# A two-layer sparse-attention trunk: values of a head pair later, softmax's last pass on ScalarE

## The chip, the cores and the metric

The kernel runs on one core of a Trainium2 chip. The metric is the device time of one execution in microseconds. TensorE does the matrix products, VectorE, ScalarE and GpSimd the elementwise work, and all DMAs of the part in question are issued from SyncE's queue (SP).

## The reference

512 positions, width 1024, two layers. Each layer norms its rows, multiplies by one wide input matrix, and sends the result through two branches: a sparse attention of 8 heads (here the change is) and a gated linear attention. Both are gated, projected up, summed, projected out, normed and added to the input. Cut to what matters:

```python
q_rope, k_slc, k_win = rope(...)                  # 8 heads in 2 groups, 64 wide
p_c = masked_softmax(q_nope @ k_cmp * scale)      # compressed keys, at most 31
p_s = masked_softmax(q_rope @ k_slc * scale)      # "selected" branch
p_w = masked_softmax(q_rope @ k_win * scale)      # "window" branch
o   = gate0 * p_c @ v_cmp + gate1 * p_s @ v_slc + gate2 * p_w @ v_win
o_nsa = o * silu(p_nz)
y   = m_nsa * (o_nsa @ w_up_nsa) + m_gla * (o_gla @ w_up_gla)
out = x + rms(y @ w_out, g_post)
```

With 512 positions there are 8 key blocks and up to 16 may be chosen, and the window is 512 wide, so both branches come to plain causal softmax over all earlier keys, with keys and values of their own.

## The kernel before

Matrices are split into a high and a low part in a short float format, and a product of two of them is three matmuls (`split3`): high by high, and the two mixed ones. Weights come by DMA into one of 3 `raw` buffers; ScalarE casts the high half (`hl`, line 153) and VectorE subtracts to get the low half (line 154), after which the raw buffer is free. They are read two blocks ahead. TensorE's instructions run in the order in which the program writes them; the orders on ScalarE, VectorE, GpSimd and SP are laid out by the framework's scheduler, which goes by priority and by its own estimate of times. Each engine then works its list off in order.

Attention goes by four **pairs** of heads, p and p + 4, and for a pair through five **blocks**: the compressed branch (`cmp_steps`, m = 0), then four of `attn_steps(p, ip, br)`: first half of the queries (ip 0) with branch 0 and 1 (m = 1, 2), second half (ip 1) with branch 0 and 1 (m = 3, 4). Such a block has two score units, i = 2 ip and 2 ip + 1, and then its value products:

- `scores`: four matmuls for 128 queries against (i + 1) x 128 keys, both heads; the unit i = 0 does both branches at once and holds the second one's result. It ends in `weigh` and `turn`.
- `weigh`, for one head at a time: VectorE adds the mask and takes the extreme of each row (line 970), ScalarE takes the exponential with its sum (line 972), VectorE takes the reciprocal (974) and multiplies each row by it and by the head's gate (975).
- `turn`: VectorE transposes 32 x 32 squares into a tile `T` (935); when both units of a block are there, SP writes `T` to DRAM (`tp`, 940) and reads it back with partitions regrouped (`PT`, four DMAs, 943).
- the value products (line 998): 8 TensorE instructions for a block of ip 0, 16 for one of ip 1, into an accumulator `acc` in a PSUM pool `ps_o` of one buffer. After the last block of a pair, line 1003 reads `acc` and multiplies by the gate, ScalarE casts the high part (1005), GpSimd subtracts for the low part (1006).

Between these, `fill(us)` writes steps of independent work into TensorE's order: the remaining query and gate projections, and the other branch's up-projections (`up`), three matmuls for 0.64 of credit. The main loop over 20 blocks writes out the order by hand: `go(n)` takes block n one step on. `PT` and `T` have tags by ip, `PT` with two buffers each, `T` with one. After the loop, `need("ug7")` writes the rest of the filler, then two gate projections of the next stage, the value products of the last pair's blocks 3 and 4, and the up-projection `un0` that reads the attention output of all four pairs in turn.

Of the kernel before, what the change touches and what calls it, by code (L numbers as in the profile page):

```python
# [9 lines left out]
F32 = mybir.dt.float32  # L10
# [3 lines left out]
AF = mybir.ActivationFunctionType  # L14
OP = mybir.AluOpType
# [6 lines left out]
NEG = -1e30  # L22
# [45 lines left out]
def trunk(ctx, tc, x, wpk, sp, gvec, cs, wa, out):  # L68
# [23 lines left out]
    def new(pl, shape=(128, 512), dt=F32, tag=None, bufs=None):  # L92
        cnt[0] += 1
        kw = {} if bufs is None else {"bufs": bufs}
        return sb[pl].tile(list(shape), dt, tag=tag or pl, name=f"{tag or pl}_{cnt[0]}", **kw)

    def ps(tag):
        cnt[0] += 1
        return psp[tag].tile([128, 512], F32, tag=tag, name=f"ps_{tag}_{cnt[0]}")
# [4 lines left out]
    mm, tp = nc.tensor.matmul, nc.tensor.transpose  # L104
    V, A, G = nc.vector, nc.scalar, nc.gpsimd
# [65 lines left out]
    def get(l, n, ahead=2):  # L171
        issue(POS[l, n] + ahead)
        return ready.pop((l, n))

    def split3(o, w, h, first, last):

        mm(o, w[0], h[0], start=first, stop=False)  # L177
        mm(o, w[0], h[1], start=False, stop=False)  # L178
        mm(o, w[1], h[0], start=False, stop=last)  # L179
# [132 lines left out]
    for l in range(L):  # L312
# [21 lines left out]
        def fill(us):  # L334
            credit[0] += us
            while credit[0] > 0.3 and queue:
                credit[0] -= step(*queue[0])

        def step(name, gen):
            try:  # L340
                return next(gen)
            except StopIteration:
                queue.pop(0)
                done.add(name)
                return 0.0

        def need(name):
            while name not in done:
                step(*queue[0])
# [3 lines left out]
        gt = new("sm", (128, 4, 24), tag="gt", bufs=1)  # L353
# [152 lines left out]
        if l == 0:  # L506
            with all_but_pe:
                ident_b, cmask, pmask, valid, gmask, kbd, vbd, hidk, hidv, cos, sin = first_stage()
# [34 lines left out]
        for t in range(2):  # L543
            o = ps("s")
# [148 lines left out]
        PR = [[None, None, None, None] for _ in range(4)]  # L693
# [37 lines left out]
        def up(f, gate, wn, src, then):  # L731
            th = []

            def sig(o):
                th.append(new("th"))
                A.activation(th[0], o, AF.Tanh, scale=0.5)

            yield from fm(l, f"{gate}{f}", hT, sig)
            w = get(l, f"{wn}{f}")
            u = ps("mm")  # L740
            for k in range(4):
                sl = slice(k * 128, (k + 1) * 128)
                split3(u, (w[0][:, sl], w[1][:, sl]), src[k], k == 0, k == 3)
                if k == 3:
                    then(th[0], u)
                yield 0.64
# [31 lines left out]
        for f in range(8):  # L778
            put(f"ug{f}", up(f, "mgg", "ug", oTg, take_ug))
# [142 lines left out]
        PT, TT, held, back, nsc = {}, {}, {}, [], [0]  # L922

        def turn(p, br, i, pps):

            ip, n = i // 2, i + 1
            r = (4 * ip + 3) * 64
            if i % 2 == 0:  # L930
                TT[p, br] = new("T", (128, 4, r), tag=f"T{ip}")
            T = TT[p, br]
            t = T[:, :, (i % 2) * i * 64:((i % 2) * i + n) * 64].rearrange("p b (j g q) -> p b j g q", j=n, g=2)
            for g in range(2):
                V.transpose(t[:, :, :, g], pps[g][:, :n * 128].rearrange("p (j b q) -> p b j q", j=n, b=4))  # L935
            if i % 2:
                cnt[0] += 1
                dr = dram.tile([128, 4, r], F32, tag=f"tp{ip}", name=f"tp_{cnt[0]}", bufs=2)
                with tc.issue_after(back[-1]) if back else nullcontext():
                    dma(dr, T)  # L940
                W = PT[p, br, ip] = new("PT", (128, 4, r), tag=f"PT{ip}")
                for b in range(4):
                    back.append(dma(W[b * 32:(b + 1) * 32], dr[:, b].rearrange("(a k) r -> k a r", a=4)).ins)

        def scores(p, i, brs):

            w = (i + 1) * 128
            ww = w * len(brs)  # L950
            both = len(brs) > 1
            nsc[0] += 1
            o = [ps("ts"[nsc[0] % 2]) for _ in range(2)]
            for g in range(2):
                for n in range(2):
                    kn = first[g][:, n].rearrange("p b n -> p (b n)") if both else keys[brs[0]][g][n][:, :w]
                    mm(o[g][:, :ww], PR[p][1][g][:, i * 128:(i + 1) * 128], kn, start=(n == 0), stop=(n == 1))  # L957
            pps = [weigh(p, g, i, brs, o[g]) for g in range(2)]
            turn(p, brs[0], i, [t[0] for t in pps])
            if both:  # L960
                held[p] = [t[1] for t in pps]

        def weigh(p, g, i, brs, o):
            h, w = p + 4 * g, (i + 1) * 128
            out = []
            for n, br in enumerate(brs):
                ob = o[:, n * w:(n + 1) * w]
                sx = new("sm", (128, 4), tag="sx", bufs=8)
                pp = new("g")
                V.tensor_tensor_reduce(pp[:, :w], ob, cmask[:, 512 - w:512], 1.0, -3 * NEG,  # L970
                                       OP.add, OP.min, sx[:, 0:1])
                A.activation(pp[:, :w], pp[:, :w], AF.Exp, bias=sx[:, 0:1], scale=-1.0,  # L972
                             accum_out=sx[:, 1:2])
                V.reciprocal(sx[:, 2:3], sx[:, 1:2])
                V.tensor_scalar(pp[:, :w], pp[:, :w], sx[:, 2:3],  # L975
                                gt[:, i, h * 3 + 1 + br:h * 3 + 2 + br], op0=OP.mult, op1=OP.mult)
                out.append(pp)
            return out

        def attn_steps(p, ip, br):  # L980
            for i in (2 * ip, 2 * ip + 1):
                if i or not br:
                    scores(p, i, (br,) if i else (0, 1))
                else:
                    turn(p, br, i, held.pop(p))
                yield

            acc, W = PR[p][3], PT[p, br, ip]
            i0 = 2 * ip
            for j in range(i0 + 2):  # L990
                for g in range(2):
                    c0 = br * 128 + g * 64
                    if j <= i0:
                        m = W[:, :, :2 * (i0 + 1) * 64].rearrange("p a (i j g q) -> p i a j g q", i=2, g=2, q=32)
                        m, w = m[:, :, :, j, g], 256
                    else:
                        m, w = W[:, :, (2 * j) * 64 + g * 32:(2 * j) * 64 + g * 32 + 32], 128
                    mm(acc[g * 64:(g + 1) * 64, (i0 + 2) * 128 - w:(i0 + 2) * 128],  # L998
                       vsw[j // 2][:, j % 2, c0:c0 + 64], m,
                       start=False, stop=(br == 1 and j == i0 + 1), skip_group_check=True)  # L1000
            if ip == 1 and br == 1:
                f_ = new("p")
                V.scalar_tensor_tensor(f_, acc, 0.5, PR[p][2], op0=OP.mult, op1=OP.mult)
                H, Lo = new("oT", dt=F32R), new("oT", dt=F32R)
                A.copy(H, f_)  # L1005
                G.tensor_tensor(Lo, f_, H.bitcast(F32), op=OP.subtract)  # L1006
                oTn[p] = (H, Lo)
            yield

        steps = []  # L1010
# [5 lines left out]
        def go(n):  # L1016
            if 0 <= n < len(steps):
                next(live[n])
# [19 lines left out]
        for n in range(len(steps)):  # L1038
            m = n % 5
            f4 = FILL[m]  # L1040
            if m == 0:
                need(f"q{steps[n][0]}")
            if m == 4:
                need(f"nz{steps[n][0]}")
            go(n)
            if m == 3:
                go(n - 5)
                go(n - 4)
            fill(f4[0])
            if m == 2:  # L1050
                go(n - 2)
            fill(f4[1])
            if m != 0:
                go(n)
                fill(f4[2])
            if m == 3:
                go(n - 3)
            if m == 4:
                go(n - 3)
                go(n - 2)  # L1060
            fill(f4[3])
        need("ug7")

        uns = [up(f, "mgn", "un", oTn, take_un(f)) for f in range(8)]
# [10 lines left out]
        src = x if l == 0 else x1  # L1075
# [6 lines left out]
        for s in range(ST):  # L1082
# [4 lines left out]
            o = [ps("s" if s % 2 and n < 2 else "mm") for n in range(len(pieces))]  # L1087
# [17 lines left out]
            for h, c0, c1 in pieces:  # L1105
                V.scalar_tensor_tensor(xh[h][:, c0:c1], tt[h][:, c0:c1], rs[:, 0:1], xh[h][:, c0:c1],  # L1106
                                       op0=OP.mult, op1=OP.add)
# [80 lines left out]
```

## Time and profile before

| what | us |
|---|---|
| median of 3 runs (lowest, highest) | 810.62 (809.73, 812.09) |
| the profiled execution's own time | 808.68 |
| its span, first to last instruction | 807.0 |
| TensorE busy | 789.5 (98%) |
| VectorE busy | 553.5 (69%) |
| ScalarE busy | 354.4 (44%) |
| GpSimd busy | 97.6 (12%) |

A matmul counts as busy from its start until its result is written, and matmuls overlap, so an engine that is 98% busy may still start its matmuls late; the distance of starts tells. The attention parts of the two layers lie at about 148 to 306 and 543 to 702 us. TensorE's granted clock was 0.997 of full speed in the mean, 1.00 in the attention parts.

### The profile page before, as it was taken

The page shows a single profiled execution, that of the slowest core. Times are in us where ns is not written, and L with a number is a line of the kernel's source. Part 1 is how long each engine was busy: PE and PEld are TensorE (multiplying, and loading weights), DVE is VectorE, ACT ScalarE, POOL GpSimd, SP SyncE. Part 2 cuts the span into 40 slices and gives each one's busy share as a digit, 9 for nine tenths or more (in the row PEclk, how much of TensorE's full clock was granted, in tenths as well). Part 3 has the DMA queues.
Part 4 walks back from the last instruction along what each step waited for, and adds up shares of the span by engine and source line. Part 5 has one row for each costly group of instructions (what it writes and reads, how often), then busy time and mean ns, then how long its engine had stood idle before and what let it go on. Part 6 is the DMA issues. An engine that isn't in the chain of part 4 may idle for free. (4 is left out here: it accounts for less than half of the span.)

```text
span 807.0 us, 12043 instructions
## 1 busy us (share of the span) xinstructions
PE 789.5 (98%) x4262; PEld 644.4 (80%) x4262; DVE 553.5 (69%) x1274; ACT 354.4 (44%) x731; POOL 97.6 (12%) x117
## 2 busy tenths in 40 slices
PE   8999999999989999999999999999999999999996
PEld 5888788887878887888898878888877788788885
DVE  6753749999998945645574366589999987366223
ACT  5671236554554524442356413556555444245211
POOL 3000024000010102211010102311000101032100
PEclk9999999999999999999999999999999999999998
DMA  6641124367676773446246121234767677545222
GB/s 233 229 147 58 53 67 130 105 191 217 183 236 204 235 227 119 153 153 223 79 129 212 52 78 54 83 114 149 223 201 215 214 212 222 171 157 158 78 105 79
DMA packets 54272, 124.04 MB, mean 154 GB/s; under 512 B 6562, under 2 KB 23490, under 8 KB 54212
## 3 DMA queue, kind: packets, MB, share of 16 engines
q1 hardware_dynamic: 54064, 123.01, 48.4%
q8 instruction: 34, 0.56, 0.3%
q10 hardware_dynamic: 148, 0.27, 0.1%
q14 instruction: 26, 0.21, 0.1%
HBM read 94.94 MB, written 25.17 MB: 149 GB/s over the span
## 5 line engine op out<-in xcount | busy, mean ns | idle before, releaser
L177 PE MATMUL ps_mm<-hT,hl 128*128 128x512 f32 x544 | 217.5, 400 | 0.0
L178 PE MATMUL ps_mm<-hT,hl 128*128 128x512 f32 x544 | 212.5, 391 | 0.0
L179 PE MATMUL ps_mm<-hT,hl 128*128 128x512 f32 x544 | 212.3, 390 | 0.0
L153 ACT CAST hl<-raw 128x1024 fp32r<-128x1024 f32 (+3 forms) x107 | 97.6, 915 | 138.3 <-PE ps_mm L178 99.9
L154 DVE TENSOR_TENSOR hl<-raw,hl 128x1024 fp32r<-128x1024 f32 (+3 forms) x107 | 117.4, 1098 | 47.6 <-ACT hl L153 42.5
L177 PEld LDWEIGHTS ps_mm<-hT,hl 128*128 128x128 f32 x544 | 102.2, 188 | 23.3 <-issue 3.1
L179 PEld LDWEIGHTS ps_mm<-hT,hl 128*128 128x128 f32 x544 | 102.2, 188 | 22.1
L178 PEld LDWEIGHTS ps_mm<-hT,hl 128*128 128x128 f32 x544 | 102.4, 188 | 19.0
L972 ACT ACTIVATE g<-g,sx 128x128 f32<-128x128 f32 (+3 forms) x128 | 71.0, 555 | 67.9 <-DVE sx L970 67.5
L935 DVE STREAM_TRANSPOSE T<-g 128x256 f32<-128x256 f32 (+3 forms) x128 | 58.6, 491 | 0.7
L975 DVE TENSOR_SCALAR g<-g,sx,gt 128x128 f32<-128x128 f32 (+3 forms) x128 | 57.0, 459 | 1.5
L178 PE MATMUL ps_mm<-oT,hl 128*128 128x512 f32 x128 | 50.3, 393 | 1.7 <-POOL oT L1006 1.7
L177 PE MATMUL ps_mm<-oT,hl 128*128 128x512 f32 x128 | 50.9, 398 | 0.0
L179 PE MATMUL ps_mm<-oT,hl 128*128 128x512 f32 x128 | 49.9, 390 | 0.0
L1006 POOL TENSOR_TENSOR oT<-p,oT 128x512 fp32r<-128x512 f32 x8 | 14.3, 1784 | 239.0 <-ACT oT L1005 239.0
L998 PE MATMUL ps_o<-PT,a 128*64 128x256 f32 (+1 forms) x384 | 38.6, 348 | 3.9 <-DMA PT<-tp 3.9
L998 PEld LDWEIGHTS ps_o<-PT,a 128*64 128x64 f32 x384 | 25.4, 137 | 18.3 <-issue 9.4
L200 POOL TENSOR_TENSOR rs<-ms,mhalf 128x1 f32<-128x1 f32 (+1 forms) x24 | 17.2, 719 | 177.0 <-DVE ms L198 175.3
L1026 POOL TENSOR_TENSOR p<-p,g 128x512 f32<-128x512 f32 x16 | 28.0, 1750 | 84.3 <-DVE p L1025 72.7
L970 DVE CUSTOM_DVE_ANT_0 g<-ps_t,cmask 128x256 f32<-128x256 f32 (+3 forms) x64 | 28.8, 477 | 2.3 <-PE ps_t L957 2.2
L970 DVE CUSTOM_DVE_ANT_0 g<-ps_s,cmask 128x128 f32<-128x128 f32 (+3 forms) x64 | 29.0, 481 | 1.7 <-PE ps_s L957 1.7
L178 PEld LDWEIGHTS ps_mm<-oT,hl 128*128 128x128 f32 x128 | 24.1, 188 | 6.5 <-POOL oT L1006 2.3
(269 smaller groups left out, 1313.3 us busy)
## 6 DMA issues: line engine op xcount, KB each, us to landing
raw<-wpk SPq DMA_DIRECT2D x96, 512.0 KB, 3.8
tp<-T SPq DMA_DIRECT2D x16, 896.0 KB, 4.1
PT<-tp SPq DMA_DIRECT2D x64, 224.0 KB, 4.9
raw<-wpk SPq DMA_DIRECT2D x32, 256.0 KB, 3.0
tp<-T SPq DMA_DIRECT2D x16, 384.0 KB, 2.5
PT<-tp SPq DMA_DIRECT2D x64, 96.0 KB, 2.4
a<-wpk SPq DMA_DIRECT2D x16, 256.0 KB, 5.7
p<-x SPq DMA_DIRECT2D x16, 256.0 KB, 2.9
```

The costliest lines, as they stand in the source:

```text
L153: A.copy(H[:, :w], r[:, :w])
L154: V.tensor_tensor(Lo[:, :w], r[:, :w], H[:, :w].bitcast(F32), op=OP.subtract)
L177: mm(o, w[0], h[0], start=first, stop=False)
L178: mm(o, w[0], h[1], start=False, stop=False)
L179: mm(o, w[1], h[0], start=False, stop=last)
L200: G.tensor_tensor(r[:, :n], ms[:, :n], mhalf[:, :n], op=OP.pow)
L935: V.transpose(t[:, :, :, g], pps[g][:, :n * 128].rearrange("p (j b q) -> p b j q", j=n, b=4))
L970: V.tensor_tensor_reduce(pp[:, :w], ob, cmask[:, 512 - w:512], 1.0, -3 * NEG, OP.add, OP.min, sx[:, 0:1])
L972: A.activation(pp[:, :w], pp[:, :w], AF.Exp, bias=sx[:, 0:1], scale=-1.0, accum_out=sx[:, 1:2])
L975: V.tensor_scalar(pp[:, :w], pp[:, :w], sx[:, 2:3], gt[:, i, h * 3 + 1 + br:h * 3 + 2 + br], op0=OP.mult, op1=OP.mult)
L998: mm(acc[g * 64:(g + 1) * 64, (i0 + 2) * 128 - w:(i0 + 2) * 128], vsw[j // 2][:, j % 2, c0:c0 + 64], m, start=False, stop=(br == 1 and j = ...
L1026: G.tensor_tensor(t_, t_, y2[f], op=OP.add)
```

## The change

It has four pieces. The main loop's order: the value products of a pair's first two `attn_steps` blocks (m = 1, 2) move from the end of its block m = 4 to the first gap of the next pair's block m = 0 (for the last pair: behind the loop); those of its last two blocks (m = 3, 4) move from behind the first score unit of the next pair's m = 3 to in front of its second score unit. `weigh` now does both heads of a unit and one branch in a call: one reciprocal and one product with the gates for both heads, on 128 x 2, and the multiplication of the rows by ScalarE (`A.mul`) in place of VectorE. The end of a pair: line 1003 gets high priority in the scheduler, and for the last pair VectorE, not GpSimd, subtracts the low part. In `up`, the product with the low half of the source comes last of the three.

```diff
@@ up
-                split3(u, (w[0][:, sl], w[1][:, sl]), src[k], k == 0, k == 3)
+                mm(u, w[0][:, sl], src[k][0], start=(k == 0), stop=False)
+                mm(u, w[1][:, sl], src[k][0], start=False, stop=False)
+                mm(u, w[0][:, sl], src[k][1], start=False, stop=(k == 3))
@@ scores, weigh
-            pps = [weigh(p, g, i, brs, o[g]) for g in range(2)]
-            turn(p, brs[0], i, [t[0] for t in pps])
+            pps = [weigh(p, i, br, [o[g][:, n * w:(n + 1) * w] for g in range(2)]) for n, br in enumerate(brs)]
+            turn(p, brs[0], i, pps[0])
             if both:
-                held[p] = [t[1] for t in pps]
-
-        def weigh(p, g, i, brs, o):
-            h, w = p + 4 * g, (i + 1) * 128
-            out = []
-            for n, br in enumerate(brs):
-                ob = o[:, n * w:(n + 1) * w]
-                sx = new("sm", (128, 4), tag="sx", bufs=8)
-                pp = new("g")
-                V.tensor_tensor_reduce(pp[:, :w], ob, cmask[:, 512 - w:512], 1.0, -3 * NEG,
-                                       OP.add, OP.min, sx[:, 0:1])
-                A.activation(pp[:, :w], pp[:, :w], AF.Exp, bias=sx[:, 0:1], scale=-1.0,
-                             accum_out=sx[:, 1:2])
-                V.reciprocal(sx[:, 2:3], sx[:, 1:2])
-                V.tensor_scalar(pp[:, :w], pp[:, :w], sx[:, 2:3],
-                                gt[:, i, h * 3 + 1 + br:h * 3 + 2 + br], op0=OP.mult, op1=OP.mult)
-                out.append(pp)
-            return out
+                held[p] = pps[1]
+
+        def weigh(p, i, br, o):
+
+            w = (i + 1) * 128
+            sx = new("sm", (128, 8), tag="sx", bufs=4)
+            pps = [new("g") for _ in range(2)]
+            for g, pp in enumerate(pps):
+                V.tensor_tensor_reduce(pp[:, :w], o[g], cmask[:, 512 - w:512], 1.0, -3 * NEG,
+                                       OP.add, OP.min, sx[:, g:g + 1])
+                A.activation(pp[:, :w], pp[:, :w], AF.Exp, bias=sx[:, g:g + 1], scale=-1.0,
+                             accum_out=sx[:, 2 + g:3 + g])
+            V.reciprocal(sx[:, 4:6], sx[:, 2:4])
+            V.tensor_mul(sx[:, 6:8], sx[:, 4:6], gt[:, i, 3 * p + 1 + br:3 * p + 14 + br:12])
+            for g, pp in enumerate(pps):
+                A.mul(pp[:, :w], pp[:, :w], sx[:, 6 + g:7 + g])
+            return pps
@@ attn_steps
                 f_ = new("p")
-                V.scalar_tensor_tensor(f_, acc, 0.5, PR[p][2], op0=OP.mult, op1=OP.mult)
+                with tc.high_priority():
+                    V.scalar_tensor_tensor(f_, acc, 0.5, PR[p][2], op0=OP.mult, op1=OP.mult)
                 H, Lo = new("oT", dt=F32R), new("oT", dt=F32R)
                 A.copy(H, f_)
-                G.tensor_tensor(Lo, f_, H.bitcast(F32), op=OP.subtract)
+                (G if p < 3 else V).tensor_tensor(Lo, f_, H.bitcast(F32), op=OP.subtract)
@@ main loop
             go(n)
+            fill(f4[0])
+            if m == 0:
+                go(n - 4)
+                go(n - 3)
+            if m == 2:
+                go(n - 2)
+            fill(f4[1])
             if m == 3:
                 go(n - 5)
                 go(n - 4)
-            fill(f4[0])
-            if m == 2:
-                go(n - 2)
-            fill(f4[1])
             if m != 0:
                 go(n)
                 fill(f4[2])
+            fill(f4[3])
             if m == 3:
                 go(n - 3)
-            if m == 4:
-                go(n - 3)
-                go(n - 2)
-            fill(f4[3])
+        go(len(steps) - 4)
+        go(len(steps) - 3)
         need("ug7")
```

## Rows read from the trace of the kernel before

**Rows 1.** Windows by pair: us; busy PE, PEld, DVE, ACT, POOL; clock, DMA.
```profile
...
174.60:211.00 36.40, 36.40 (x200) 29.11 (x199) 34.66 (x105) 18.78 (x48) 2.85 (x2) 1.00 0.73 214
...
211.00:249.60 38.60, 36.54 (x200) 29.32 (x199) 36.50 (x110) 19.46 (x49) 2.15 (x1) 1.00 0.66 209
...
605.10:643.40 38.30, 36.43 (x200) 29.19 (x199) 36.31 (x110) 19.84 (x50) 2.16 (x1) 1.00 0.66 212
...
```

**Rows 2.** Waits of TensorE, whole span: us in total, times, longest us.
```profile
...
PE ps_o L998 <- DMA PT<-tp: 3.9, 2, 2.1
...
PE ps_mm L178 <- POOL oT L1006: 1.7, 2, 0.8
...
```

**Rows 3.** Timeline of one weight block: start, us, engine, line, operation.
```profile
...
209.34 1.03 ACT L153 CAST hl<-raw 128x1024 fp32r<-128x1024 f32 x1
...
213.95 1.22 DVE L154 TENSOR_TENSOR hl<-raw,hl 128x1024 fp32r<-128x1024 f32 x1
...
218.71 0.40 PE L177 MATMUL ps_mm<-hT,hl 128*128 128x512 f32 x1
...
```

**Rows 4.** Timeline of SP's queue, 207 to 226 us.
```profile
...
207.58 8.00 SPq L136 DMA_DIRECT2D raw<-wpk  x2
...
215.68 1.80 SPq L943 DMA_DIRECT2D PT<-tp  x4
...
225.40 1.80 SPq L943 DMA_DIRECT2D PT<-tp  x4
...
```

**Rows 5.** Timeline of TensorE and VectorE around the first wait.
```profile
...
232.29 1.74 PE L998 MATMUL ps_o<-PT,a 128*64 128x256 f32 x16 [2.06 <-DMA PT<-tp]
...
235.44 0.65 DVE L1003 SCALAR_TENSOR_TENSOR p<-ps_o,oT 128x512 f32<-128x512 f32 x1
...
239.78 0.39 PE L918 MATMUL ps_o<-p,vbd 128*128 128x512 f32 x1
...
```

**Rows 6.** VectorE: line 975 in three periods, then groups by shape.
```profile
...
sum 111.40, DVE 21.82; mean DVE 7.27
...
L975 DVE TENSOR_SCALAR g<-g,sx,gt 128x512 f32<-128x512 f32 x16 | 8.3, 531 | 0.1
...
L974 DVE RECIPROCAL sx<-sx 128x1 f32<-128x1 f32 x64 | 9.4, 155 | 3.4 <-ACT g L972 3.2
...
L726 DVE TENSOR_TENSOR oT<-p,oT 128x512 fp32r<-128x512 f32 x3 | 2.1, 684 | 0.0
...
```

**Rows 7.** ScalarE groups by shape: count, busy us, mean ns, idle before.
```profile
...
L972 ACT ACTIVATE g<-g,sx 128x512 f32<-128x512 f32 x16 | 11.5, 717 | 8.0 <-DVE sx L970 8.0
...
L972 ACT ACTIVATE g<-g,sx 128x128 f32<-128x128 f32 x16 | 6.2, 391 | 6.2 <-DVE sx L970 6.2
...
L698 ACT ACTIVATE a<-ps_mm 128x512 f32<-128x512 f32 x3 | 1.7, 580 | 0.0
...
```

**Rows 8.** Timelines of three engines at the last pair's end, first layer.
```profile
...
303.11 3.25 PE L998 MATMUL ps_o<-PT,a 128*64 128x256 f32 x32
...
308.01 0.39 PE L178 MATMUL ps_mm<-oT,hl 128*128 128x512 f32 x1
...
308.23 0.39 PE L179 MATMUL ps_mm<-oT,hl 128*128 128x512 f32 x1
...
308.52 0.50 PE L177 MATMUL ps_mm<-oT,hl 128*128 128x512 f32 x1
...
309.87 0.50 PE L178 MATMUL ps_mm<-oT,hl 128*128 128x512 f32 x1 [0.84 <-POOL oT L1006]
...
307.13 0.69 DVE L1003 SCALAR_TENSOR_TENSOR p<-ps_o,oT 128x512 f32<-128x512 f32 x1
...
308.54 1.27 POOL L1006 TENSOR_TENSOR oT<-p,oT 128x512 fp32r<-128x512 f32 x1 [33.40 <-ACT oT L1005]
...
```

**Rows 9.** DMA issues: count, KB each, median us to landing.
```profile
...
tp<-T SPq DMA_DIRECT2D x8, 896.0 KB, 4.1
...
PT<-tp SPq DMA_DIRECT2D x32, 224.0 KB, 5.0
...
```

## The prediction

> **What bounds the kernel now.** I read the stretches by head pair first, then the list of who TensorE waits for, then the order of time around each of its waits, on the DMA queue, VectorE and ScalarE, and last the durations of the operations that move. In the attention part each pair takes a period of 36.40 us in which TensorE shows 36.40 us busy; VectorE is busy for 34.66 us of it, 95%, and ScalarE for 18.78 us, 52% [rows 1]. One period of each layer is longer: 38.60 us, with 36.54 us busy, in the first and 38.30 us in the second [rows 1]. So TensorE is the bound, and a change to the softmax is worth only the TensorE waits that it takes away. The list has two kinds inside attention: the value products of line 998 for the transposed weights that come back from memory, 3.9 us in two waits, and the up-projection for the low half of the attention output that GpSimd makes on line 1006, 1.7 us in two [rows 2]. That is the whole ground to be won.
>
> The first wait goes back to VectorE. The high half of a weight block is ready when ScalarE's 1.03 us from 209.34 end, at 210.4; VectorE begins the low half only at 213.95, because it is working off softmax [rows 3]. SP's queue is in order: from 207.58 to 215.58 it stands at two weight loads that need a raw buffer which that low half, ending at 215.17, frees. Only then, at 215.68, does it issue the loads of the transposed weights for branch 0 of the pair's second half of queries, and at 225.40 those for branch 1 [rows 4]. The value products of that branch 1 start at 232.29, after 2.06 us of waiting [rows 5].
>
> **The change part by part.** *Softmax's last pass.* VectorE loses line 975, 7.27 us per period in the mean [rows 6]. Of 16 reciprocals of 155 ns per period [rows 6] 8 stay, each for two heads, and 8 products on 128x2 come. At this size the start-up is all there is, so I price a product as a reciprocal, and the two cancel; twice that would add 1.2 us. VectorE goes from 34.66 to about 27.5 us, 75% of the period. ScalarE gets 16 multiplications per period by a factor that differs by partition, four of each width from 128 to 512. The trace has none; the nearest are its multiplication by a constant, 580 ns at 512, and the exponential that also reads a value per partition, 717 ns at 512 and 391 at 128 [rows 7]. The upper bound is the exponential's, a mean of 554 ns: 16 x 0.554 = 8.9 us. The lower takes 580 ns at 512 and the exponential's slope, 109 ns per 128 columns: 4 x (580 + 471 + 362 + 254) ns = 6.7 us. I take 8.9 because of the operand. ScalarE then has 18.78 + 8.9 = 27.7 us, 76% of the period. Neither passes TensorE's 36.40, so this part costs TensorE nothing by itself; what hides it is the filler work between score units.
>
> The Trainium skill (ScalarE: Activation LUTs, "Rules for kernel authors") speaks against this part: it wants multiplications on VectorE. On one instruction the rows agree, 531 ns for line 975 at 512 columns against 580 to 717 [rows 6, 7]. By that page's formula ("What ACT_TABLE_LOAD costs": 186 ns + 0.833 ns per column, and 93 ns for a pointer operand), an estimate for 16 passes at a mean of 320 columns is 8.7 us, which leaves the sum as it is.
>
> *Latency of a unit.* The chain was sums, exponential, reciprocal, scaling, transposes, head by head; now both heads' exponentials come before one reciprocal, then a product (about 0.16), then ScalarE and back. Two passes of at most 0.72 replace two of about 0.53, and one head waits for the other: about 1 us more in an idle machine (an estimate from [rows 6, 7]). A gain is possible too, since VectorE's backlog, 3.6 us in the case above, shrinks.
>
> *Values later.* The same 16 and 32 value products run, no more and no fewer group changes, and no DMA is added. A pair's first units go from the end of its last block to the first gap of the next pair, 2.6 us of filler and the compressed scores later. The last ones go 1.5 + 1.2 = 2.7 us of filler later in the fourth block of the next pair. Against a wait of 2.06 us this alone, less the 1 us of latency, leaves 0.3 us; the shorter backlog, which freed the raw buffer 3.6 us late, takes more than that. I take the wait as gone: 3.9 us [rows 2]. The bounds are 0 (the next part, rival B) and 3.9.
>
> What may be late next is the accumulator, of which there is one: a new pair's first product on it (239.78) must follow the read of line 1003, which ended at 236.1 [rows 5]. After the change only four scores (4 x 0.23 us) and 3.3 us of filler, about 4.3 us, lie between. In the old order the read began 1.4 us after the products ended and took 0.65, so 2.2 us of cover stay, and the raised priority adds to them. I cost it at nothing; if VectorE is over 2.2 us late, every excess is TensorE's.
>
> *The end of the last pair.* TensorE's matmuls in a row start 0.22 to 0.23 us apart (308.01, 308.23); here one starts at 308.52 and the next at 309.87, 1.35 us later, so 1.12 us are lost per layer, more than the 0.84 shown as idle, because a matmul's pipeline still counts as busy [rows 8]. The low half took GpSimd 1.27 us from 308.54. VectorE's same operation takes 0.68 [rows 6]: from 308.5 it ends near 309.2. The reordered up-projection asks for it one matmul later, at 308.98, so 0.2 us stay at worst. If priority puts line 1003 ahead of the split that it stood behind, it starts near 306.4, not 307.13, and nothing stays. Gain per layer 0.9 to 1.12; I take 1.0, two layers 2.0 us. The reorder needs the low half of the weights 0.23 us earlier; the tightest one seen, ready at 215.2 and used at 218.71, has 3.5 us [rows 3].
>
> **Sum.** 3.9 + 2.0 = 5.9 us. The profiled execution took 808.68 us, of which its span is 807.0, so it would take 802.8; its time lies 1.94 below the median of the runs, 810.62. For the median I forecast 810.62 - 5.9 = 804.7 us.
>
> **The rivals.** *B: the wait is refilled.* The transposed weights travel twice, 896 KB out in 4.1 us and four pieces back in 5.0 [rows 9], with weights on the same queue. If these transfers, not VectorE, set the landing, or the longer unit and its tiles held longer (12 slots, eight of which fill with the other branch's results during attention) eat the 2.7 us, the value products wait as before and only the 2.0 us of the end are won: 808.6. For it speaks that branch 1's loads went out from 225.40 on and were needed at 230.2, less than the 5.0 of one load; against it that SP stood 8 us for a buffer.
>
> *C: ScalarE becomes the bound (slower).* Its instructions run in order. A multiplication now waits for VectorE's reciprocal and product, and weight casts, tanh and the next exponentials stand behind it; who waits for them is first VectorE's low halves, then SP, then TensorE. ScalarE's spare time is 36.4 - 27.7 = 8.7 us per period, 1.1 us for each of 8 units. If each unit holds it 1.3 us, a period grows by 1.6 us, 8 periods by 13: 810.6 + 13 - 5.9 = 818. Beyond 1.23 us per unit the kernel is slower by more than 0.3%. Against it: VectorE has a quarter of its time free after the change, and tight weights have 3.5 us. The Trainium skill (TensorE: Matmul & The Clock Gate, "Architectural detail") has ScalarE's and VectorE's queues as strict first in, first out, which is the condition of this rival. If it holds, the rule of the Trainium skill's page on ScalarE, named above, is right for the kernel as a whole.
>
> **How the numbers follow.** 0.3% is 2.4 us, about what a measurement of this kernel can tell from no change. My forecast has 0.70: its own range is 802 to 807 (all of 3.9 + 2.2 gained and some of the runs' 1.94, or a third of the waits left). B has 0.19, from 808.6 to 811, within 0.3%. C has 0.11, above 811. So 802 to 811 leaves out C and a small part below. Faster 0.70, same 0.19, slower 0.11.
>
> **What would show it.** Right: no wait of line 998 for the loads above 0.3 us, all periods 36.4 us; the wait for the low half under 0.3 us; VectorE near 27.5 and ScalarE near 27.7 us per period; multiplications of about 0.7 us at 512; SP's long stand at weight loads shorter. Wrong: TensorE waits for weight halves or for the accumulator, or periods longer than 36.4 with ScalarE above 90%.

## The result, and the profile after

The changed kernel takes 804.91 us in the median of four runs (804.62 to 805.33), the kernel before 810.45 in four (809.73 to 812.09): a ratio of 0.9931 [0.9915, 0.9947], 5.5 us less. The forecast was 804.7, 5.9 us less. The profiled execution took 805.33 us, with a span of 803.6.

The total came out; its parts did not. The waits of TensorE, whole span (total us, times, longest us):

```profile
PE ps_o L999 <- DMA PT<-tp: 1.7, 2, 1.0
...
PE ps_o L920 <- DVE p L1005: 0.2, 1, 0.2
```

The wait for GpSimd's low half is gone, and so are the two of about 2 us [rows 2]. But value products still wait for transposed weights, in another place, and the accumulator, which I had priced at nothing, is waited for. The load by stretches of about one pair, first layer (us; busy PE, PEld, DVE, ACT, POOL; clock, DMA):

```profile
172.10:209.05 36.95, 36.73 (x200) 29.27 (x199) 29.89 (x83) 24.08 (x60) 2.59 (x2) 1.00 0.63 189
209.05:246.35 37.30, 36.60 (x200) 29.23 (x199) 29.13 (x92) 27.92 (x69) 1.30 (x1) 1.00 0.70 211
246.35:282.60 36.25, 36.25 (x200) 29.17 (x199) 28.19 (x87) 26.50 (x65) 1.30 (x1) 1.00 0.80 243
sum 110.50, PE 109.58 PEld 87.67 DVE 87.22 ACT 78.50 POOL 5.19; mean PE 36.53 PEld 29.22 DVE 29.07 ACT 26.17 POOL 1.73
```

Beside [rows 1], VectorE fell to 29.07 us per stretch and ScalarE rose to 26.17. TensorE has 0.92 us idle in the three, 0.22 and 0.70; both places follow. Groups by shape (count, busy us, mean ns, idle before) of the new work, beside [rows 6, 7]:

```profile
L978 ACT ACTIVATE g<-g,sx 128x512 f32<-128x512 f32 x32 | 21.4, 715 | 6.3 <-DVE sx L976 6.3
...
L978 ACT ACTIVATE g<-g,sx 128x256 f32<-128x256 f32 x32 | 14.5, 500 | 4.0 <-DVE sx L976 3.9
...
L976 DVE TENSOR_TENSOR sx<-sx,gt 128x2 f32<-128x2 f32 x64 | 12.0, 188 | 1.4
```

A multiplication by ScalarE costs 715 ns at 512 columns: the exponential's 717, which I took as the upper bound. An estimate by the formula of the Trainium skill (ScalarE: Activation LUTs, "What ACT_TABLE_LOAD costs") is 706 ns, and 492 at 256 columns; the trace, with 715 and 500, agrees within 10 ns.

**Where TensorE still waits.** Value products of a pair's blocks m = 1 and 2, now in the next pair's first gap (start, us, engine, line, operation):

```profile
202.82 0.47 PE L920 MATMUL ps_o<-p,vbd 128*128 128x512 f32 x1 [0.22 <-DVE p L1005]
...
212.29 0.87 PE L999 MATMUL ps_o<-PT,a 128*64 128x256 f32 x8
213.86 0.87 PE L999 MATMUL ps_o<-PT,a 128*64 128x256 f32 x8 [0.70 <-DMA PT<-tp]
```

SP's queue, from which the load of those weights comes:

```profile
202.12 0.34 SPq L942 DMA_DIRECT2D tp<-T  x1
202.50 6.24 SPq L136 DMA_DIRECT2D raw<-wpk  x2
208.85 1.79 SPq L945 DMA_DIRECT2D PT<-tp  x4
```

The write of the tile went out at 202.12 and landed 2.5 us later, at 204.60. The load back went out only at 208.85: SP stood at two weight loads for 6.24 us, over 4 us of them after the landing. From 208.85 to the second eight products at 213.86 are 5.0 us. In the kernels below that do not wait here, the second eight start 0.70 us after the first; here that would have been at 212.99, 4.1 us after the load went out. ScalarE and VectorE in that time:

```profile
205.33 1.34 ACT L978 ACTIVATE g<-g,sx 128x512 f32<-128x512 f32 x2 [0.49 <-DVE sx L976]
...
207.05 0.61 ACT L153 CAST hl<-raw 128x512 fp32r<-128x512 f32 x1
```

```profile
202.01 0.65 DVE L1005 SCALAR_TENSOR_TENSOR p<-ps_o,oT 128x512 f32<-128x512 f32 x1
...
207.69 0.69 DVE L154 TENSOR_TENSOR hl<-raw,hl 128x512 fp32r<-128x512 f32 x1 [0.28 <-ACT hl L153]
```

Read backwards: SP's second weight load goes out when VectorE has made a low half (207.69 to 208.38). VectorE waited 0.28 us for ScalarE's high half of the same block, which ScalarE made at 207.05, after the two multiplications of a unit and a tanh; the multiplications had themselves waited 0.49 us for VectorE's product. This is rival C's chain, on the small scale of 0.70 us. The first row of VectorE is the accumulator: the products of the pair before ended at 197.34 and its read began at 202.01, 4.7 us later, where I had counted 1.4.

**The end of the last pair**, TensorE, then VectorE, beside [rows 8]:

```profile
306.92 0.50 PE L743 MATMUL ps_mm<-oT,hl 128*128 128x512 f32 x1
...
307.25 0.40 PE L744 MATMUL ps_mm<-oT,hl 128*128 128x512 f32 x1
...
307.64 0.50 PE L745 MATMUL ps_mm<-oT,hl 128*128 128x512 f32 x1
```

```profile
304.32 1.29 DVE L148 TENSOR_TENSOR a<-raw,a 128x512 fp32r<-128x512 f32 x2
...
305.52 0.69 DVE L1005 SCALAR_TENSOR_TENSOR p<-ps_o,oT 128x512 f32<-128x512 f32 x1
...
306.89 0.69 DVE L1008 TENSOR_TENSOR oT<-p,oT 128x512 fp32r<-128x512 f32 x1 [0.69 <-ACT oT L1007]
```

Matmuls start 0.33 and 0.39 us apart where 0.23 is the rule, and the one before these, at 306.63, was followed 0.29 us later: some 0.3 us are left of 1.12. The low half is VectorE's at 0.69 us. Line 1005 still stands behind the split of line 148. The program as laid out has the same instructions in the same order on every engine with and without the raised priority, so that line of the change does nothing.

### The profile page after: what moved, and what is told of

Its sections match the earlier page's. It is cut to its first block, busy times and chain, and to the rows that moved or that the text cites. A ratio compares the mean times of both kernels' runs of the same rounds, so it can differ in the third digit from the quotient of the medians.

```text
span 803.6 us, 12013 instructions
## 1 busy us (share of the span) xinstructions
PE 788.8 (98%) x4262; PEld 643.5 (80%) x4262; DVE 514.4 (64%) x1148; ACT 410.1 (51%) x859; POOL 91.9 (11%) x115
## 5 line engine op out<-in xcount | busy, mean ns | idle before, releaser
L973 ACT ACTIVATE g<-g,sx 128x128 f32<-128x128 f32 (+3 forms) x128 | 70.6, 553 | 28.8 <-DVE sx L971 28.6
L978 ACT ACTIVATE g<-g,sx 128x128 f32<-128x128 f32 (+3 forms) x128 | 64.1, 553 | 18.4 <-DVE sx L976 16.3
L745 PEld LDWEIGHTS ps_mm<-oT,hl 128*128 128x128 f32 x128 | 24.0, 188 | 6.0 <-DVE oT L1008 0.9
L743 PEld LDWEIGHTS ps_mm<-oT,hl 128*128 128x128 f32 x128 | 24.0, 188 | 5.3 <-ACT oT L1007 0.6
```

Source lines behind the costliest of these rows:

```text
L743: mm(u, w[0][:, sl], src[k][0], start=(k == 0), stop=False)
L745: mm(u, w[0][:, sl], src[k][1], start=False, stop=(k == 3))
L973: A.activation(pp[:, :w], pp[:, :w], AF.Exp, bias=sx[:, g:g + 1], scale=-1.0, accum_out=sx[:, 2 + g:3 + g])
L978: A.mul(pp[:, :w], pp[:, :w], sx[:, 6 + g:7 + g])
```

## The experiments

**1 to 4. The pieces apart.** Before with only the reordered `up` and the low half by VectorE:

```diff
-                split3(u, (w[0][:, sl], w[1][:, sl]), src[k], k == 0, k == 3)
+                mm(u, w[0][:, sl], src[k][0], start=(k == 0), stop=False)
+                mm(u, w[1][:, sl], src[k][0], start=False, stop=False)
+                mm(u, w[0][:, sl], src[k][1], start=False, stop=(k == 3))
...
-                G.tensor_tensor(Lo, f_, H.bitcast(F32), op=OP.subtract)
+                (G if p < 3 else V).tensor_tensor(Lo, f_, H.bitcast(F32), op=OP.subtract)
```

> The kernel before with only the end of a pair changed (VectorE subtracts the last pair's low half, priority on the read of the accumulator, low half of the source last in the up-projection). Theory M (gain = TensorE waits taken away, each by its own piece): the waits for the low half, 1.12 us a layer, fall to about 0.2, the waits for the transposed weights stay at about 3.9 us; ratio to before about 0.9975 (-2.0 us). Rival S (the end is hidden anyway, its wait was paid by a later one): 1.000. If the whole gain came from here: 0.993.

Before with only the new main loop:

```diff
+            if m == 0:
+                go(n - 4)
+                go(n - 3)
...
-            if m == 4:
-                go(n - 3)
-                go(n - 2)
```

> The kernel before with only the order of the main loop changed: values later, softmax and the end as before. Theory M: 2.7 us of filler against a wait of 2.06, and no longer chain in a unit, so the waits for transposed weights go to under 0.5 us in all: -3.5 us, ratio 0.9957; the waits of 1.12 us for the low half stay. Rival R (the backlog of VectorE is what makes the loads late, and the order alone does not cure it): the waits stay above 2 us in all, some at a new place, the first units' values: -1 us, 0.999.

Before with only the new `weigh` (two heads in a call, `A.mul`):

> The kernel before with only the new softmax (last pass on ScalarE, two heads together): values at their old places. Theory M: about 1 us longer chain of a unit against a shorter backlog; the waits for transposed weights come to between 0 and 4 us in all, near 2, that is -2 us, 0.9975. Rival R (the backlog is the cause): the waits go, -3.9 us, 0.995. Rival L (latency: the longer unit makes every value group late): waits grow at several places, +3 us or more, 1.004.

The changed kernel with the old `weigh`, that is the loop and the end together:

> The changed kernel without the new softmax: order and end as changed, last pass of softmax on VectorE. Theory M: positions do most of it, so it is as fast as the changed kernel within 1 us: -5.5 us, 0.9932. Rival R: the waits for transposed weights stay above 2 us: about -3 us, 0.9963.

| kernel | median us | ratio to before [95%] | waits for transposed weights, us |
|---|---|---|---|
| end alone | 808.96 | 0.9982 [0.9968, 0.9997] | 4.4 |
| order alone | 803.31 | 0.9916 [0.9900, 0.9932] | none |
| softmax alone | 810.43 | 1.0008 [0.9990, 1.0026] | 4.4 |
| order and end, old softmax | 801.94 | 0.9900 [0.9884, 0.9916] | none |
| all (the change) | 804.91 | 0.9931 [0.9915, 0.9947] | 1.7 |

Order alone is worth 810.46 - 803.31 = 7.1 us, the end 1.5, the softmax alone nothing; with the other two the softmax costs 3.0 us. Before, in these runs, is 810.46. The kernel with order and end alone beats the changed one. Three of the four forecasts by theory M missed: it had 0.9957 for the order, 0.9975 for the softmax and 0.9932 for order and end together; only the end, forecast at 0.9975, came out near. For the softmax neither rival fits either (0.995 and 1.004).

TensorE's instructions come in the same order in the changed kernel and in that one, so the starts of the same instruction can be laid side by side. This is the place of the wait in the kernel with the old softmax, on TensorE, SP, ScalarE and VectorE:

```profile
212.49 1.52 PE L1000 MATMUL ps_o<-PT,a 128*64 128x256 f32 x16
```

```profile
200.93 0.34 SPq L942 DMA_DIRECT2D tp<-T  x1
201.31 5.34 SPq L136 DMA_DIRECT2D raw<-wpk  x2
206.75 1.79 SPq L945 DMA_DIRECT2D PT<-tp  x4
```

```profile
203.61 0.60 ACT L153 CAST hl<-raw 128x512 fp32r<-128x512 f32 x1
```

```profile
205.63 0.65 DVE L154 TENSOR_TENSOR hl<-raw,hl 128x512 fp32r<-128x512 f32 x1
```

Here all 16 products run without a gap, the second eight from 213.19. ScalarE casts at 203.61, right behind its exponentials, not at 207.05; the low half starts at 205.63, not at 207.69; the load goes out at 206.75, not at 208.85. The tile itself is written 1.2 us earlier. Start by start, the changed kernel loses 0.96 us at 213.86 and 1.27 at the same place of the second layer, 0.46 and 0.30 at the accumulator and 0.32 at one more set of products: 3.3 us, of which 0.7 had been gained in the first 33 us of the program, and the spans differ by 2.8. Nothing else in TensorE's order moved.

**5 and 6. Which half of the new softmax costs.** First the pair of heads stays together, but VectorE multiplies; then ScalarE multiplies, but one head at a time (shown against the `weigh` of before):

```diff
-                A.mul(pp[:, :w], pp[:, :w], sx[:, 6 + g:7 + g])
+                V.tensor_scalar(pp[:, :w], pp[:, :w], sx[:, 6 + g:7 + g], None, op0=OP.mult)
```

> The changed kernel with one edit: the last pass of softmax runs on VectorE again, the sums of two heads still together. The changed kernel gave 0.9931, order and end without the new softmax 0.9900, so the new softmax costs about 3 us. Theory E (the pass on ScalarE costs them, by its longer chain): 0.990. Rival P (the common reciprocal costs them, since one head waits for the other): 0.993. VectorE back near 34 us a period.

```diff
-                V.tensor_scalar(pp[:, :w], pp[:, :w], sx[:, 2:3],
-                                gt[:, i, h * 3 + 1 + br:h * 3 + 2 + br], op0=OP.mult, op1=OP.mult)
+                V.tensor_mul(sx[:, 3:4], sx[:, 2:3], gt[:, i, h * 3 + 1 + br:h * 3 + 2 + br])
+                A.mul(pp[:, :w], pp[:, :w], sx[:, 3:4])
```

> The changed kernel with one edit: each head by itself again (own reciprocal, own product with the gate), the last pass still on ScalarE. Theory E: 0.993, with waits for transposed weights of 1 to 2 us in all. Rival P: 0.990 and no such waits.

Both take 802.06 us, 0.9898 [0.9867, 0.9929] and 0.9892 [0.9856, 0.9928]: neither half alone costs anything. The first result fits theory E, the second rival P, so neither theory is right by itself. From the issue of that load to the start of the second eight products are 5.1 us (207.10 to 212.24) with pairs on VectorE, 11.2 (201.75 to 212.94) with single heads on ScalarE, 6.4 (206.75 to 213.19) with the old softmax, and in the changed kernel there would have been 4.1 (208.85 to 212.99), where a load then took 5.0. A load costs nothing as long as this margin is longer than the load.

Pairs on VectorE are the clean comparison: SP issues the same transfers in the same order as in the changed kernel, and only the engine of the last pass differs. So at this place the pass on ScalarE takes 1.0 us of margin, and that is what TensorE then waits for. With single heads SP's list is another one: its load stands behind weight loads for only 2.28 us (199.37 to 201.65). That run shows that multiplications on ScalarE need not cost anything, but not that pairing the heads is what makes them cost.

**7. Still later.** If lateness of the loads is all, products put later still should not wait. The products of m = 1 and 2 go one gap later, and those of the compressed branch (m = 0), which start the new pair's accumulator, from the end of block m = 3 into block m = 4:

```diff
-            if m == 0:
-                go(n - 4)
-                go(n - 3)
             if m == 2:
                 go(n - 2)
+            if m == 4:
+                go(n - 4)
             fill(f4[1])
+            if m == 0:
+                go(n - 4)
+                go(n - 3)
...
-            if m == 3:
-                go(n - 3)
```

> The changed kernel with two steps moved further back: the values of a pair's first units one gap later in the next pair (1.6 us of filler), the start of the new pair's accumulator one block later. Theory N (the new softmax costs only what is seen as waits there: 1.7 us for transposed weights, 0.4 us for the accumulator, and what varies with them between runs): all of these go, 802 us, 0.990 to 0.991. Rival: it costs TensorE elsewhere too, or the waits move on: 0.993.

A miss: 816.28 us, 1.0069 [1.0043, 1.0096]. The old places no longer wait, but two new waits of 4.9 and 4.7 us stand at the products of the second half. SP and then TensorE:

```profile
219.74 0.34 SPq L942 DMA_DIRECT2D tp<-T  x1
222.30 6.36 SPq L136 DMA_DIRECT2D raw<-wpk  x2
228.77 1.79 SPq L945 DMA_DIRECT2D PT<-tp  x4
```

```profile
236.85 3.26 PE L999 MATMUL ps_o<-PT,a 128*64 128x256 f32 x16 [4.91 <-DMA PT<-tp]
```

Again SP stands at two weight loads, 6.36 us, between the write of a tile and its load back. But this is not the whole wait. The write issued at 219.74 landed only at 226.95, after 7.2 us, so SP's stand, which ended at 228.66, held the load back by 1.8 us beyond that; the load itself then took 8.1 us, where it took 5.0 in the changed kernel. Moving the products moved the steps of the scheduler's list too, and with them which loads stand in front of which.

**8. The price of rival C.** Every multiplication by ScalarE is done a second time into a spare tile that nobody reads:

```diff
+        spare = new("const", (128, 512), BF, tag="spare")
...
                 A.mul(pp[:, :w], pp[:, :w], sx[:, 6 + g:7 + g])
+                A.mul(spare[:, :w], pp[:, :w], sx[:, 6 + g:7 + g])
```

> The changed kernel with each multiplication of the last pass run a second time by ScalarE into a spare tile that nobody reads: 16 more passes of 0.55 us a period, 8.9 us, off the chain of the unit but in ScalarE's order. ScalarE goes from about 26 to 35 of 36.9 us. Rival C of the prediction (beyond some spare time ScalarE's order of work makes it the bound): slower than before, 1.01 or more. Theory M (ScalarE has room to its last us): as the changed kernel, 0.993 to 0.996.

812.59 us, 1.0031 [1.0013, 1.0049], which is 7.7 us above the change. TensorE's waits, and the first two stretches of the table above:

```profile
PE ps_o L920 <- DVE p L1008: 4.7, 4, 1.4
PE ps_mm L914 <- DVE g L910: 3.0, 2, 1.5
...
PE ps_o L1002 <- DMA PT<-tp: 1.1, 2, 0.8
```

```profile
172.10:209.05 36.95, 33.95 (x187) 26.67 (x186) 25.96 (x79) 29.60 (x74) 2.59 (x2) 1.00 0.65 194
209.05:246.35 37.30, 35.93 (x198) 28.52 (x197) 27.57 (x84) 32.68 (x78) 1.29 (x1) 1.00 0.67 200
```

(The stretches are the same times as above, not quite the same work.) ScalarE at 80 and 88% of a stretch makes TensorE wait for the accumulator's read and for the compressed branch. Rival C is real, though smaller than its forecast of 1.01 or more: its price here is 7.7 us for some 5 us more of ScalarE's time per stretch. In the change itself, with ScalarE at 71%, the accumulator is waited for 0.22 us and no wait for the compressed branch is listed.

**9 to 12. Is it SP's order?** Theory Q, formed after these: what is late is not VectorE's or ScalarE's work on softmax but SP, which stands at a weight load for a raw buffer while a load of transposed weights, whose tile is long written, is queued behind it. Then GpSimd, nearly idle, can issue the weight loads. First the kernel before, where the loads of the attention part's filler go over:

```diff
-        dma(r[:, :w], src)
+        (nc.gpsimd.dma_start if n.startswith(("q", "nz", "mgg", "ug")) else dma)(r[:, :w], src)
```

> The kernel before with one edit: the weight loads of the attention part are issued by GpSimd, not by SP, so that no load of transposed weights can stand behind one. Theory Q (the loads come late because they stand in SP's queue behind weight loads that wait for a raw buffer): SP issues each of them as soon as its tile is written out, and the two waits of 2 us shrink to under 0.5 us each: about -3 us, 0.996. Rival T (the transfers themselves are slow, or VectorE's backlog delays the tile): the waits stay, 1.000, or it is slower by what GpSimd's own order delays.

805.21 us, 0.9925 [0.9910, 0.9940], with the order and the softmax of before. SP, and the products that waited 2.06 us in [rows 5]:

```profile
217.00 0.34 SPq L940 DMA_DIRECT2D tp<-T  x1
221.53 2.17 SPq L943 DMA_DIRECT2D PT<-tp  x4
```

```profile
PE ps_mm L178 <- POOL oT L1006: 1.7, 2, 0.8
...
PE ps_o L998 <- DMA PT<-tp: 0.2, 1, 0.2
```

The load goes out 4.5 us after its tile's write, where it took 7.2 before (218.18 to 225.40), and 3.9 us earlier than in [rows 4]; the wait goes from 3.9 to 0.2 us, while that for GpSimd's low half, which the edit does not touch, stays. No softmax and no order of TensorE changed, so moving weight loads off SP is enough to take these waits away; the gain, 6.4 us, is twice what Q forecast. The way, though, is not only the one that Q names. SP in the kernel before:

```profile
218.18 0.34 SPq L940 DMA_DIRECT2D tp<-T  x1
219.09 6.20 SPq L136 DMA_DIRECT2D raw<-wpk  x2
```

The packets of this write ran from 220.58 to 224.72, so the stand until 225.29 held the load back by 0.6 us at most. They began 2.4 us after the issue, while the loads back of branch 0, which SP's first stand had kept until 215.68 [rows 4], were still on their way (packets from 217.18 to 222.38). In experiment 9 those loads go out at 209.43, and the write's packets run from 217.84 to 221.02. So by these times SP's order acts here through transfers that meet, and rival T is half right.

The same edit on the changed kernel, then with the first three blocks of the next stage's gate and up weights (`mgn0` to `mgn2`, `un0` to `un2`) too, then that on the kernel of experiment 7:

> The changed kernel with the same edit. Theory Q: the waits of 0.7 and 1.0 us at the first units' values go, since SP's stand of 6 us at weight loads was between the tile's landing and its load back; the new softmax then costs nothing that TensorE sees: about 802 us, 0.990. Rival T: the waits stay, 0.993 or slower.

> As the run before on the changed kernel, but with the next stage's first weight loads (mgn and un, 0 to 2) on GpSimd too: there SP stood 9.8 us at one of them ahead of the load that TensorE then waited 2.5 to 2.7 us for. Theory Q: with no weight load left between a tile's write and its load back, both waits go: 802 us, 0.990 to 0.991. Rival T (the new softmax delays the tile itself by more than the order gives): waits of over 1 us stay, 0.994 or more.

> The kernel that moved values and accumulator further back and came out at 1.007, with the same weight loads on GpSimd. Theory Q: its waits of 4.9 and 4.7 us came from SP standing 6.4 us at weight loads and not from the positions; they go, and with them the stretch at the lower TensorE clock: 0.990 to 0.992. Rival (the later positions themselves cost): above 1.000.

They take 809.14 us (0.9974 [0.9959, 0.9988]), 807.50 (0.9949 [0.9931, 0.9968]) and 807.92 (0.9951 [0.9931, 0.9971]). All stay well above the 801.94 of experiment 4, which Q alone would have given if nothing else had stood in SP's way. In the first, the wait at 213.86 is gone, but one of 2.5 us stands at 272.45: a weight load that SP still issues waits for its buffer from the write of the tile on (the tile landed at 257.53):

```profile
254.01 0.34 SPq L942 DMA_DIRECT2D tp<-T  x1
264.04 0.35 SPq L136 DMA_DIRECT2D raw<-wpk  x1
264.50 1.79 SPq L945 DMA_DIRECT2D PT<-tp  x4
```

With the `mgn` and `un` blocks on GpSimd too, the last place is the last pair's, behind a weight load that SP kept (the packets of the write ended at 290.18):

```profile
284.56 0.34 SPq L942 DMA_DIRECT2D tp<-T  x1
296.37 0.35 SPq L136 DMA_DIRECT2D raw<-wpk  x1
296.87 1.94 SPq L945 DMA_DIRECT2D PT<-tp  x4
```

That is its only wait for transposed weights, 2.0 us in each layer. At the place where the changed kernel waits, Q shows directly: with SP free, the load goes out 0.06 us after its tile has landed, at 203.22.

```profile
200.94 0.34 SPq L942 DMA_DIRECT2D tp<-T  x1
203.28 1.73 SPq L945 DMA_DIRECT2D PT<-tp  x4
```

Up to the last pair's wait, in the first layer, every TensorE instruction starts within 0.25 us of the same one in experiment 4: with SP free, the new softmax costs nothing. The rest of its distance, 4.7 us of span, is those two waits and a lower clock behind the second (last section). The late kernel of experiment 7 loses its 4.9 us waits with the same edit (816.28 to 807.92) and keeps only the last pair's.

So Q names the cause of the changed kernel's waits for transposed weights, and of those left in experiments 10 to 12, where a load went out 4 to 7 us after its tile had landed; in the kernel before and in experiment 7 the times say that transfers that met did most of it. Its forecasts of about 802 us for experiments 10 to 12 missed all the same, because SP kept weight loads that were not thought of. Nor does every stand cost something: in experiment 4 one of 5.34 us lies between the write and the load, and TensorE does not wait.

## Why the prediction was right, and where it was not

**The total** held by luck, because two errors cancel: the order was worth more than forecast, and the softmax, forecast to help it, cost 3.0 us. By the prediction's own signs it was not right throughout: waits of 0.70 and 1.0 us for the loads stand where none above 0.3 was to be, and the accumulator is waited for.

*Order.* Forecast 3.9 us, measured 7.1 alone, with an interval from 5.5 to 8.1. The waits gone are those that I had; two things beside them were left out of the sum. A wait costs a little more than its idle time: at 232.29 TensorE falls 2.2 us behind experiment 9, with 2.06 shown. Between the profiled executions of before and of the order alone, the two waits make 4.3 us. And a wait of this length now and then takes the clock down behind it (last section). The profiled execution of before had escaped that: its clock stayed at 1.00 behind both waits, and it lay 1.8 us below the later runs' median (808.68 against 810.46). An estimate from the mean clocks, 0.996 over before's 23 runs against 0.998, is 1.6 us. I had seen such a distance, 1.94, and put it into the range only; with the waits it goes too. The two come to 5.9 us. What is left of the 7.1 stays open: in the first 104 us, ahead of the attention part, the profiled executions of all kernels scatter by 1.9 us.

*The step that failed* is "Neither passes TensorE's 36.40, so this part costs TensorE nothing by itself", with its companion, the shorter backlog that "takes more than that". VectorE's relief did come, but TensorE had no use for it: alone it brought the load of the second half's branch 1 from 225.40 to 224.34, its products still waited 2.05 us, and the time did not move. The prediction had read its backlog of 3.6 us at the stand before branch 0's load. The stand that ends just before branch 1's load, the one waited for, is the second one (219.09 to 225.29, shown in experiment 9). The low half that ended it began at 223.74, only 0.34 us after its high half was ready, so there was hardly a backlog to shorten. With the new order there was no wait left to help, and the latency, which I had at 1 us and did count against the old place, was spent at a place that I had not looked at, the pair's first units in the next pair's gap. There the tile was written 1.2 us later, the high half of a weight block was 3.4 us later on ScalarE, and 6.4 us of margin became 4.1 where the load took 5.0.

*ScalarE.* The multiplication was priced right, 715 ns against 717. Per stretch ScalarE stands at 26.17 us, forecast 27.7, and VectorE at 29.07, forecast 27.5. Against the kernel with the same order and the old softmax (18.93 and 34.58) that is +7.2 and -5.5, where my sums were +8.9 and -7.2: instructions in a row overlap (two multiplications of 715 ns take 1.34 us), so sums of durations run high on both sides. Nothing hung on it.

*The accumulator.* The cover of 2.2 us was counted from a read 1.4 us after the products; it came 4.7 us after, behind VectorE's softmax and weight work, and 0.22 us of wait are shown in the first layer. The raised priority, which I added to the cover, moved nothing.

*The end.* Forecast 2.0 us for both layers, measured 1.5 alone, with an interval from 0.2 to 2.6; some 0.3 us per layer stay, as line 1005 was not moved up.

*The rivals.* B was half right: the wait was refilled, at 1.7 instead of 3.9 us, in the changed kernel not by the transfers' own time but by SP's standing. C's chain is what refilled it: with the pass back on VectorE and SP's list unchanged it is gone (experiment 5), and experiment 8 shows how it grows. That SP stood 8 us was in [rows 4], and I used it against rival B instead of asking which of the loads behind it would be next.

*What stays open.* Moving the weight loads to GpSimd also shifts instructions on other engines a little, since the scheduler lays out its lists anew, and in their traces the loads issued by GpSimd go by another DMA queue than SP's; so experiments 9 to 12 do not change SP's order alone. The kernel of experiment 4 with this edit, which would show what the edit costs by itself, was not run. A fourth raw buffer, which would free SP in another way, does not fit the memory and was not tried. How much of the spread of before is the clock behind its two waits rests on the mean clock of each run; the one execution of before with a trace had no such fall.

## What to carry to other kernels

When a queue that issues loads in order stands at one for want of a buffer, look for the load behind it that somebody will need next, and measure the margin from its issue to its use against the time that such a load takes; a change that eats margin costs nothing up to that point and everything beyond it. Look too for the write ahead of such a load: it can be late behind transfers that were held back earlier. An engine that is not the bound gains nothing from relief, but what is put on another one's list delays all that stands behind it, here a weight cast that frees the buffer. Run the pieces of a change apart: this one holds one worth 7.1 us, one worth 1.5 and one that takes 3.0 back.

## What the runs showed of the hardware

A wait of TensorE can cost the clock behind it. Stretches behind waits of 4.9 us (experiment 7, with the one that holds the wait) and of 2.0 us (experiment 11, first and second layer); the column before the last two is the granted clock:

```profile
229.00:236.80 7.80, 2.94 (x22) 1.80 (x20) 3.93 (x10) 4.03 (x9) 0.00 (x0) 0.91 0.98 260
236.80:240.00 3.20, 3.15 (x16) 1.94 (x16) 1.16 (x4) 0.00 (x0) 0.00 (x0) 0.50 0.39 112
```

```profile
304.27:307.00 2.73, 2.73 (x21) 2.12 (x22) 0.69 (x1) 0.23 (x1) 0.00 (x0) 1.00 0.66 252
697.36:700.00 2.64, 2.64 (x17) 1.89 (x18) 0.20 (x1) 0.00 (x0) 0.00 (x0) 0.67 0.70 258
700.00:701.60 1.60, 1.60 (x5) 1.22 (x5) 0.92 (x2) 0.62 (x1) 0.00 (x0) 0.50 0.04 17
```

After 4.9 us the clock is at 0.50, the 1.2 GHz level, and 16 products take 3.26 us instead of 1.74 [rows 5]. In experiment 11 it stayed at 1.00 behind the wait in the first layer and fell behind an equally long one in the second, where TensorE lost 1.2 us more against experiment 4. Over the attention parts and ends of pairs in all the traces, the clock fell at both waits of more than 4 us, at 5 of the 12 of 1.9 to 2.7 us, and at none of the 17 of 0.6 to 1.5 us. Length alone does not decide among the 12: it fell behind 1.95 us (experiment 1) and not behind 2.5 us (experiment 10).

This fits the spread of a kernel with such waits. In its 69 runs beside the experiments before took from 807.29 to 815.23 us, with a mean clock of 0.991 to 0.999; the 24 runs at 0.994 or lower took 812.5 us in the mean, the 22 at 0.997 or higher 809.1, and it is the same way round in each of the four sets in which they were taken. With the order alone all four runs had 0.998 and lay within 0.45 us.

The other surprise is the load itself: with the DMA engines 98% busy at 260 GB/s (first row above), a load of transposed weights took 8.1 us from issue to products in experiment 7. It took 6.9 in the kernel before (225.40 to 232.29; 93%, 255 GB/s) and 5.0 at the changed kernel's place (87%, 283 GB/s). So the time that a load needs is read at its own place; which of the other transfers made it long was not told apart.

That a DMA waits at its issuer and not in its queue is also in the Trainium skill (DMA: Bandwidth & Descriptors, "Anatomy of one DMA — SWDGE (gpsimd) path"): a semaphore is waited for by the issuing sequencer before the DMA is handed on. The section follows a DMA that GpSimd issues; the trace shows the same of SP: in the changed kernel SP stood at line 136 until 208.74, and the load behind it, whose tile had landed at 204.60, went out at 208.85.
